# Layer 0's last two groups of MLP tiles by seven quarter products, the modulation columns moved between the groups, and a new order of the seven

## The chip, the cores and the metric

One core of a Trainium2 chip runs the whole kernel. The metric is the device time of one execution in microseconds; the core's five engines are TensorE (PE in the profile), VectorE (DVE), ScalarE (ACT), GpSimd (POOL) and SyncE (SP, which issues all loads here). Each engine works through its own list of instructions in the order in which the list was written, and waits on semaphores for the others.

## The reference, cut to what matters

Two layers, each with a mixer and an MLP, over a sequence of 512 positions of width 1024 in float32. The change touches the MLP and the modulation vectors that both sub-layers use:

```python
for l in range(DEPTH):
    mod = c_act @ w_ada[l] + b_ada[l]              # 6 vectors of 1024 per layer
    ...
    h = rms_norm(x, g_pre_mlp[l]) * (1 + sc_mlp) + sh_mlp
    f = jnp.square(jax.nn.relu(h @ w_ff1[l])) @ w_ff2[l]   # 1024 -> 4096 -> 1024
    x = x + gt_mlp * rms_norm(f, g_post_mlp[l])
```

## The kernel before, in words

Activations lie transposed: 128 features on the partitions, 512 positions along the row. A float32 product is made of three passes in a rounded format: every operand is split into a high part (a cast on ACT) and a low part (the difference, on DVE or POOL), and `passes` (L193 to L200) issues high x high (L198), high x low (L199) and low x high (L200). One block of weights is 128 x 1024 and serves eight 128 x 128 pieces, so a tile of 128 outputs from 1024 inputs is 24 matmuls of 512 columns. `wblock` loads a block (`raw`), casts it on ACT (`whi`, L190) and subtracts on POOL (`wlo`, L191); four buffers `w` hold two blocks' high and low parts.

The MLP (function `mlp`) goes through the 32 tiles of the first product in groups. After the tiles of a group (ff1) comes the second product over just these tiles (ff2): eight tiles `y[m]`, which the first group writes and the later ones add to. `f_out` (L788 to L793) turns a tile into its squared relu and splits it: relu on ACT (L790), square on DVE (L791), high part on ACT (L792), low part on DVE (L793). The bank of PSUM that held the tile is free for PE after L793. There are three banks `mm`, two `cv`, two `ax` and one `cx`.

In layer 0 there are two groups of 16 tiles, all plain. In layer 1 there are four groups of 8, and groups 1 to 3 take their tiles in pairs by `pair_out`: a Strassen-Winograd scheme with seven products of quarter size (256 columns, four 128-blocks deep, 12 matmuls each, so 84 per pair) in place of eight. Its inputs are seven combinations of the quarters of the pair's weights, made by DVE and POOL and split into `wq` tiles (in the same four `w` buffers), and combinations of the activations' quarters, `ta` and `tb`, which `quarters` (L799 to L815) makes once, on DVE, behind the last first-product tile of the group before; its reads and sums go L804 to L810, its split through L174 (ACT) and L175 (DVE). In `pair_out` the banks are `bx` (products w1, then w2 onto it), `ba` (w6), `bb` (w5, then w3 onto it) and `bc` (w7, then w4 onto it); `p1`, `u2` and `q5` are the running sums (L851, L853, L855), and four calls of `f_out` end the pair.

Beside the layer 0 MLP the kernel makes 56 columns of the modulation vectors on DVE: `some(n)` pops n of them, and `ada_col` loads 128 x 1024 numbers (`adr`, three buffers) and reduces them against `cbc` (L293), always behind the last instruction noted in `last[0]`. Before, a first-product tile has one column beside it and a second-product tile two. The last eight second-product tiles' last block is left to `finish`, whose weights are loaded ahead into `slot` buffers (25 in all, one of them held by `cbc` until the last column).

The order on each engine comes from a scheduler with priorities; blocks of weights carry a higher priority (`WPRI`), so their casts are placed early among the other work of ACT. `behind` adds an order without a semaphore.

Of the kernel before, what the change touches and what calls it, by code (L numbers as in the profile page):

```python
# [53 lines left out]
def trunk(ctx, tc, xT, vecs, bg, cst, ccol, crow, wadn, wadt, win, win0, wqkv, wgate, wout, wff1, wff2, yT):  # L54
# [17 lines left out]
    NB = 7  # L72
    GROUPS = [[(16, (1, 2)), (16, (1, 2))], [(8, (0, 0))] * 4]
    SEVEN = [9, 1]
    S2 = 5
# [711 lines left out]
    def mlp(l, hp, pre):  # L787
# [28 lines left out]
        def wq(src, lo_eng):  # L816
            t = wpool.tile([P, 2, T], F32, name="wq", tag="w", bufs=WBUF)
            split(t, src, lo_eng=lo_eng)
            return t

        def pair_out(m, pm, pm1):

            with tc.high_priority(offset=WPRI):
# [11 lines left out]
                w5 = wq(s1, dve)  # L835
                w2 = wq(a12, pool)
                s3, s4 = s2(), s2()
                pool.tensor_tensor(s3, a11, a21, op=ALU.subtract)
                w7 = wq(s3, pool)
                dve.tensor_tensor(s4, a12, s2p, op=ALU.subtract)  # L840
                w3 = wq(s4, pool)
                w4 = wq(a22, pool)

# [11 lines left out]
            dve.tensor_tensor(q5, bb, u2, op=ALU.add)  # L855
            prod(bx, w2, hp[4:8], h0, True)
            f_out(bx, pm, h0)
            prod(bc, w7, ta, h1)
            dve.tensor_tensor(ba, bc, q5, op=ALU.add)
            f_out(ba, pm1, h1)  # L860
            prod(bb, w3, hp[4:8], h1, True)
            dve.tensor_tensor(bb, bb, u2, op=ALU.add)
            f_out(bb, pm, h1)
            prod(bc, w4, tb, h1, True)
            dve.tensor_tensor(bc, bc, u2, op=ALU.add)
            f_out(bc, pm1, h0)

        y, base = None, 0
        for g, (size, rate) in enumerate(GROUPS[l]):
            fp = []  # L870
            if g == 0:
# [6 lines left out]
            for m in range(len(fp), size):  # L878
                if g >= SEVEN[l]:
                    if m % 2 == 0:  # L880
                        fp += [slot(), slot()]
                        pair_out(base + m, fp[-2], fp[-1])
                        some(rate[0])
                else:
                    o = gemm([wff1[l, base + m]], hp)
                    fp.append(slot())
                    f_out(o, fp[-1], slice(0, T))
                    some(rate[0])
            if g == SEVEN[l] - 1:
# [5 lines left out]
            if len(parts):  # L895
                for m in range(NF):
# [3 lines left out]
                    else:  # L900
                        last[0] = dve.tensor_tensor(y[m], y[m], o, op=ALU.add)
                    some(rate[1])
            base += size
# [118 lines left out]
```

## Time and profile before

| | us |
|---|---|
| median of 3 runs | 1593.04 (1591.09 to 1594.87) |
| profiled execution | 1588.86 |
| its span | 1587.1 |
| PE busy | 1525.5 (96%) |
| DVE / ACT / POOL busy | 966.9 / 730.6 / 833.4 |
| mean granted clock | 0.988 |

The span is what the trace covers, from the first to the last instruction; 1.8 us of the execution lie outside. The MLP of layer 0 lies at about 460 to 820 us, that of layer 1 at about 1225 to 1580 us.

### The profile page before, as it was taken

To read this page: it belongs to the slowest core of one execution; us is meant where nothing else is said; L and a number is where in the kernel's file an instruction comes from. 1 tells how busy PE (TensorE), PEld (TensorE's weight loads), DVE (VectorE), ACT (ScalarE), POOL (GpSimd) and SP (SyncE) were. 2 spreads that over 40 slices of the span, in tenths; PEclk is the share of its full clock that TensorE was granted. 3 is DMA by queue.
4 is the path that set the end of the run, shared out by engine and by line. 5 is a ranking of instruction groups with operands and counts; after the bars stand their busy time and mean duration, and the time that the engine had idled before them with its cause. 6 is when DMAs were issued, how large, how long until landed. Compare 5 with 4: busy or idle time off the path is not lost.

```text
span 1587.1 us, 22583 instructions
## 1 busy us (share of the span) xinstructions
PE 1525.5 (96%) x8452; PEld 1268.4 (80%) x8452; DVE 966.9 (61%) x1969; ACT 730.6 (46%) x1308; POOL 833.4 (53%) x536
## 2 busy tenths in 40 slices
PE   5999999999999999999999999999999999999997
PEld 4776766678998888888899777676899879898897
DVE  6899998742363521447667999997316356253544
ACT  3364753454463322332463665445355446253462
POOL 0275753256744444445872867335674446464672
PEclk9999999999999999999999999999999999999999
DMA  8524323303413555566630222220241223333241
GB/s 320 189 81 153 133 90 133 133 27 107 146 57 118 186 200 177 194 189 233 228 107 8 80 73 80 93 67 27 93 144 56 81 93 94 97 95 113 82 134 54
DMA packets 56278, 189.00 MB, mean 119 GB/s; under 512 B 6376, under 2 KB 8552, under 8 KB 56168
## 3 DMA queue, kind: packets, MB, share of 16 engines
q1 hardware_dynamic: 56168, 187.56, 35.8%
q8 instruction: 66, 1.08, 0.3%
q14 instruction: 44, 0.36, 0.1%
HBM read 185.44 MB, written 2.10 MB: 118 GB/s over the span
## 4 chain that ended last, share of the span: by engine, by line
PE 77%; DVE 3%; ACT 2%; POOL 1%; issue 1%; DMA 0%; POOLq 0%; ACTq 0%
PE ps_mm L198 23%; PE ps_mm L200 23%; PE ps_mm L199 23%; PE ps_mm L684 2%; PE ps_mm L696 2%; PE ps_ax L338 1%; POOL wlo L191 1%; ACT whi L190 1%; PE ps_ax L266 1%; PE ps_ax L600 0%; PE ps_ax L671 0%; PE ps_ax L364 0%; DVE ps_cv L451 0%; PE ps_ax L725 0%; PE ps_cv L199 0%
## 5 line engine op out<-in xcount | busy, mean ns | idle before, releaser
L191 POOL TENSOR_TENSOR wlo<-raw,whi 128x1024 fp32r<-128x1024 f32 (+1 forms) x192 | 440.8, 2297 | 436.5 <-ACT whi L190 414.8
L198 PE MATMUL ps_mm<-slot,whi 128*128 128x512 f32 (+1 forms) x1440 | 546.5, 381 | 7.3 <-ACT slot L174 3.4
L200 PE MATMUL ps_mm<-slot,wlo 128*128 128x512 f32 (+1 forms) x1440 | 546.6, 380 | 4.8 <-POOL wlo L191 4.7
L199 PE MATMUL ps_mm<-slot,whi 128*128 128x512 f32 (+1 forms) x1440 | 545.2, 379 | 0.0
L190 ACT CAST whi<-raw 128x1024 fp32r<-128x1024 f32 (+1 forms) x192 | 191.2, 996 | 417.4 <-PE ps_mm L199 304.9
L451 DVE SCALAR_TENSOR_TENSOR ps_cv<-slot,vv,ps_cv 128x512 f32<-128x512 f32 x480 | 332.5, 747 | 1.5
L198 PEld LDWEIGHTS ps_mm<-slot,whi 128*128 128x128 f32 x1440 | 271.7, 189 | 67.0 <-issue 4.2
L200 PEld LDWEIGHTS ps_mm<-slot,wlo 128*128 128x128 f32 x1440 | 271.4, 188 | 63.7 <-POOL wlo L191 7.9
L199 PEld LDWEIGHTS ps_mm<-slot,whi 128*128 128x128 f32 x1440 | 271.9, 189 | 58.8 <-issue 5.5
L198 PE MATMUL ps_mm<-slot 128*128 128x256 f32 (+1 forms) x568 | 160.5, 294 | 11.4 <-DVE slot L793 9.2
L199 PE MATMUL ps_mm<-slot 128*128 128x256 f32 (+1 forms) x568 | 162.9, 291 | 0.6 <-DVE slot L944 0.5
L200 PE MATMUL ps_mm<-slot 128*128 128x256 f32 (+1 forms) x568 | 162.4, 290 | 0.0
L791 DVE TENSOR_TENSOR ps_mm<-rl,ps_mm 128x256 f32<-128x256 f32 (+1 forms) x90 | 45.2, 504 | 130.4 <-ACT rl L790 130.3
L198 PEld LDWEIGHTS ps_mm<-slot 128*128 128x128 f32 x568 | 107.1, 192 | 15.0 <-DVE slot L793 10.2
L199 PEld LDWEIGHTS ps_mm<-slot 128*128 128x128 f32 x568 | 109.3, 193 | 3.2 <-DVE slot L944 0.9
L200 PEld LDWEIGHTS ps_mm<-slot 128*128 128x128 f32 x568 | 109.0, 192 | 1.0
L191 POOL TENSOR_TENSOR slot<-raw,slot 128x1024 fp32r<-128x1024 f32 x34 | 86.1, 2559 | 15.6 <-issue 10.1
L166 POOL TENSOR_TENSOR small<-small,mhalf 128x4 f32<-128x4 f32 (+1 forms) x38 | 34.1, 898 | 95.6 <-DVE small L165 90.9
L198 PE MATMUL ps_mm<-slot,wq 128*128 128x256 f32 x288 | 81.1, 283 | 3.1 <-ACT sq L851 3.1
L199 PE MATMUL ps_mm<-slot,wq 128*128 128x256 f32 x288 | 80.2, 280 | 0.0
L200 PE MATMUL ps_mm<-slot,wq 128*128 128x256 f32 x288 | 80.1, 281 | 0.0
L293 DVE CUSTOM_DVE_ANT_0 adr<-adr,cbc,ini 128x1024 f32<-128x1024 f32 x40 | 65.8, 1657 | 22.9 <-DMA adr<-in_wadt 22.9
(249 smaller groups left out, 2220.0 us busy)
## 6 DMA issues: line engine op xcount, KB each, us to landing
raw<-in_wff SPq DMA_DIRECT2D x138, 512.0 KB, 3.6
raw<-in_win SPq DMA_DIRECT2D x58, 512.0 KB, 3.2
adr<-in_wadt SPq DMA_DIRECT2D x56, 512.0 KB, 4.5
raw<-in_wout SPq DMA_DIRECT2D x36, 512.0 KB, 3.6
adr<-in_wadn SPq DMA_DIRECT2D x28, 512.0 KB, 3.9
raw<-in_wqkv SPq DMA_DIRECT2D x24, 256.0 KB, 2.7
slot<-in_wadt SPq DMA_DIRECT2D x8, 512.0 KB, 8.7
raw<-in_win SPq DMA_DIRECT2D x8, 384.0 KB, 7.0
```

The lines of the kernel that those rows point to most:

```text
L166: pool.tensor_tensor(y, u, mhalf[:, 0:n], op=ALU.pow)
L190: act.copy(out=r32(hi), in_=raw)
L191: wlast[0] = (lo_eng or pool).tensor_tensor(r32(lo), raw, hi, op=ALU.subtract)
L198: pe.matmul(out, whi, xh, start=first, stop=False, skip_group_check=more)
L199: pe.matmul(out, whi, xl, start=False, stop=False, skip_group_check=more)
L200: mark[0] = pe.matmul(out, wlo, xh, start=False, stop=last, skip_group_check=more)
L266: pe.matmul(bk[32 * g:32 * g + 32, :], cc[:, k:k + 1].broadcast_to([P, 32]), raw[:, j * T:(j + 1) * T], start=(k < 4), stop=(k >= 4), skip ...
L293: red = dve.tensor_tensor_reduce(raw, raw, cbc, scale, 0.0 if one else ini, ALU.mult, ALU.add, m)
L451: dve.scalar_tensor_tensor(acc, at[i][:, k:k + T], w, acc, op0=ALU.mult, op1=ALU.add)
L684: pe.matmul(sc[:, 0:n], kf[h][:, k, i * P:(i + 1) * P], qf[h][:, k, i * P:T], start=(k == 0), stop=(k == 1))
L696: pe.matmul(o[:, 0:DH + 1], sts[i][:, (j - i) * P:(j - i + 1) * P], vtok[h][:, i, :], start=(i == 0), stop=(i == j))
L791: dve.tensor_tensor(o, rl[:, ts], o, op=ALU.mult)
```

## The change

Layer 0 gets four groups of 8 tiles too; its groups 2 and 3 (16 tiles, eight pairs) go through `pair_out`, and `quarters` runs behind group 1's first product. Each group carries lists of how many columns stand beside each of its tiles: group 0 two beside the one plain tile behind the halves and two beside each of its eight second-product tiles, group 1 two beside each first-product tile and 2, 1, 1, 1, 1, 1, 1, 1 beside the second product's, group 2 none beside the pairs and 2, 2, 2, 2, 2, 2, 1 beside the second product's, group 3 none. In `pair_out`, in both layers, the products are written in the order w1, w6, w5, w7, w2, w4, w3 instead of w1, w6, w5, w2, w7, w3, w4, and POOL's low parts in a matching order.

```diff
-    GROUPS = [[(16, (1, 2)), (16, (1, 2))], [(8, (0, 0))] * 4]
-    SEVEN = [9, 1]
+    GROUPS = [[(8, [2], [2] * 8), (8, [2] * 8, [2] + [1] * 7), (8, [], [2] * 6 + [1]), (8, [], [])], [(8, [], [])] * 4]
+    SEVEN = [2, 1]
...
-                w2 = wq(a12, pool)
                 s3, s4 = s2(), s2()
                 pool.tensor_tensor(s3, a11, a21, op=ALU.subtract)
                 w7 = wq(s3, pool)
                 dve.tensor_tensor(s4, a12, s2p, op=ALU.subtract)
+                w2 = wq(a12, pool)
+                w4 = wq(a22, pool)
                 w3 = wq(s4, pool)
-                w4 = wq(a22, pool)
...
-            prod(bx, w2, hp[4:8], h0, True)
-            f_out(bx, pm, h0)
             prod(bc, w7, ta, h1)
             dve.tensor_tensor(ba, bc, q5, op=ALU.add)
             f_out(ba, pm1, h1)
+            prod(bx, w2, hp[4:8], h0, True)
+            f_out(bx, pm, h0)
+            prod(bc, w4, tb, h1, True)
+            dve.tensor_tensor(bc, bc, u2, op=ALU.add)
+            f_out(bc, pm1, h0)
             prod(bb, w3, hp[4:8], h1, True)
             dve.tensor_tensor(bb, bb, u2, op=ALU.add)
             f_out(bb, pm, h1)
-            prod(bc, w4, tb, h1, True)
-            dve.tensor_tensor(bc, bc, u2, op=ALU.add)
-            f_out(bc, pm1, h0)
```

On ACT, at the passage from the second to the third pair of layer 1's group 1, these rows stand in the kernel before (`rl` is a relu, `wq` a weight's high part, `sq` the copy p1; `ps_mm_12035` is bb and `ps_mm_12036` bc of the second pair, `ps_mm_12186` bx of the third, and `raw_12152` gives w2 of the third):

```order
L790 ACTIVATE rl_12127<-ps_mm_12035 128x256
L174 CAST wq_12170<-raw_12152 128x512
L174 CAST wq_12176<-s2_12173 128x512
L851 COPY sq_12190<-ps_mm_12186 128x256
L790 ACTIVATE rl_12145<-ps_mm_12036 128x256
L792 CAST slot_11997<-ps_mm_12035 128x256
L174 CAST wq_12180<-s2_12174 128x512
L792 CAST slot_11998<-ps_mm_12036 128x256
```

and these in the changed one, at the same passage (`ps_mm_12748` is bc and `ps_mm_12747` bb of the second pair, `wq_12885` is w7 and `wq_12889` w2 of the third):

```order
L174 CAST wq_12885<-s2_12882 128x512
L790 ACTIVATE rl_12839<-ps_mm_12748 128x256
L174 CAST wq_12889<-raw_12864 128x512
L790 ACTIVATE rl_12857<-ps_mm_12747 128x256
L792 CAST slot_12710<-ps_mm_12748 128x256
L792 CAST slot_12709<-ps_mm_12747 128x256
L174 CAST wq_12892<-raw_12865 128x512
L851 COPY sq_12902<-ps_mm_12898 128x256
```

The last relu of a pair and both its high parts now stand behind the next pair's cast of w2, whose buffer was w6's of that same next pair; the copy p1 stands behind them all, where it stood ahead of one relu and both high parts.

On DVE at the same passage, before:

```order
L791 TENSOR_TENSOR ps_mm_12035<-rl_12127,ps_mm_12035 128x256
L833 TENSOR_TENSOR ps_cx_12310<-ps_ax_12309,raw_12305 128x512
L791 TENSOR_TENSOR ps_mm_12036<-rl_12145,ps_mm_12036 128x256
L853 TENSOR_TENSOR sq_12191<-ps_cv_12187,sq_12190 128x256
L793 TENSOR_TENSOR slot_11997<-ps_mm_12035,slot_11997 128x256
L793 TENSOR_TENSOR slot_11998<-ps_mm_12036,slot_11998 128x256
```

and in the changed kernel:

```order
L791 TENSOR_TENSOR ps_mm_12748<-rl_12839,ps_mm_12748 128x256
L833 TENSOR_TENSOR ps_cx_13022<-ps_ax_13021,raw_13017 128x512
L791 TENSOR_TENSOR ps_mm_12747<-rl_12857,ps_mm_12747 128x256
L793 TENSOR_TENSOR slot_12710<-ps_mm_12748,slot_12710 128x256
L793 TENSOR_TENSOR slot_12709<-ps_mm_12747,slot_12709 128x256
L853 TENSOR_TENSOR sq_12903<-ps_cv_12899,sq_12902 128x256
```

The two last low parts (L793) still stand behind both squares (L791); what has changed is which bank comes first, bc now, and that PE's third product of the next pair, w5 now, is the one that is written into the bank that bc leaves (before, that place in PE's list was w2's, into bx's own bank, and w5 came fourth).

On ACT beside the second product of layer 0's group 1, before (its last tiles; `whi` is a block of ff2, `slot` from `raw` a block for `finish`):

```order
L190 CAST whi_6213<-raw_6212 128x1024
L190 CAST whi_6251<-raw_6250 128x1024
L190 CAST whi_6289<-raw_6288 128x1024
L190 CAST whi_6327<-raw_6326 128x1024
L190 CAST slot_6440<-raw_6439 128x1024
L190 CAST whi_6365<-raw_6364 128x1024
L190 CAST slot_6446<-raw_6445 128x1024
L190 CAST slot_6452<-raw_6451 128x1024
L190 CAST whi_6403<-raw_6402 128x1024
```

and in the changed kernel beside group 1's ff2 (`slot` from `ps_ax` or `ps_cx` is a high part of `quarters`; `whi_5491`, `whi_5526`, `whi_5561` and `whi_5596` are the blocks of y tiles 4, 5, 6 and 7):

```order
L174 CAST slot_5292<-ps_ax_5286 128x512
L190 CAST whi_5491<-raw_5490 128x1024
L174 CAST slot_5295<-ps_cx_5287 128x512
L190 CAST whi_5526<-raw_5525 128x1024
L174 CAST slot_5308<-ps_ax_5302 128x512
L174 CAST slot_5311<-ps_cx_5303 128x512
L174 CAST slot_5324<-ps_ax_5318 128x512
L190 CAST whi_5561<-raw_5560 128x1024
L174 CAST slot_5327<-ps_cx_5319 128x512
L830 COPY ps_ax_5635<-raw_5632 128x512
L174 CAST slot_5340<-ps_ax_5334 128x512
L174 CAST slot_5343<-ps_cx_5335 128x512
```

The casts of ff2's blocks, which stood behind one another alone, now stand behind casts that wait for what DVE makes in `quarters`; on DVE these operations stand among the columns' reductions and the additions to y.

## Rows read from the trace of the kernel before

**Rows 1.** The page: busy time by engine, and the chain that ended last by engine.

```profile
PE 1525.5 (96%) x8452; PEld 1268.4 (80%) x8452; DVE 966.9 (61%) x1969; ACT 730.6 (46%) x1308; POOL 833.4 (53%) x536
...
PE 77%; DVE 3%; ACT 2%; POOL 1%; issue 1%; DMA 0%; POOLq 0%; ACTq 0%
```

**Rows 2.** The waits of PE over the whole span: engine, tile and line that waited, what released it, microseconds in total, times, the longest.

```profile
PE ps_mm L198 <- DVE slot L793: 9.2, 5, 2.9
PE ps_mm L200 <- POOL wlo L191: 4.7, 5, 2.1
...
PE ps_mm L198 <- ACT sq L851: 3.1, 3, 1.0
```

**Rows 3.** Busy time of the engines in two stretches: layer 0's group 1, second product with two columns per tile, and one group of four pairs in layer 1 (stretch, length, busy time with the count of instructions for PE, PEld, DVE, ACT, POOL, granted clock, share of the DMA engines, GB/s).

```profile
724.00:770.00 46.00, 43.85 (x196) 35.32 (x195) 41.82 (x39) 13.34 (x15) 33.18 (x11) 1.00 0.78 272
1312.30:1353.60 41.30, 40.27 (x337) 39.82 (x336) 26.01 (x60) 28.17 (x63) 29.22 (x22) 1.00 0.33 103
```

**Rows 4.** Timeline of ACT at two plain first-product tiles of layer 0.

```profile
501.29 1.05 ACT L190 CAST whi<-raw 128x1024 fp32r<-128x1024 f32 x1 [3.25 <-PE ps_mm L199]
502.24 0.59 ACT L790 ACTIVATE rl<-ps_mm 128x512 f32<-128x512 f32 x1
503.60 0.59 ACT L792 CAST slot<-ps_mm 128x512 fp32r<-128x512 f32 x1 [0.76 <-DVE ps_mm L791]
...
507.80 0.59 ACT L790 ACTIVATE rl<-ps_mm 128x512 f32<-128x512 f32 x1
```

**Rows 5.** Timeline of PE at the second pair of layer 1's group 1 (start, duration, instruction, in brackets the idle time before it and its releaser).

```profile
1324.94 0.28 PE L200 MATMUL ps_mm<-slot,wq 128*128 128x256 f32 x1
1326.25 0.38 PE L198 MATMUL ps_mm<-slot,wq 128*128 128x256 f32 x1 [1.03 <-ACT sq L851]
1326.47 0.28 PE L199 MATMUL ps_mm<-slot,wq 128*128 128x256 f32 x1
...
1327.53 0.28 PE L199 MATMUL ps_mm<-slot,wq 128*128 128x256 f32 x1
```

**Rows 6.** Timeline of PE at the last tile of group 1's second product in layer 0.

```profile
765.49 0.28 PE L199 MATMUL ps_mm<-slot 128*128 128x256 f32 x1
767.88 0.50 PE L200 MATMUL ps_mm<-slot,wlo 128*128 128x512 f32 x1 [2.10 <-POOL wlo L191]
768.21 0.39 PE L198 MATMUL ps_mm<-slot,whi 128*128 128x512 f32 x1
```

**Rows 7.** Timeline of PE at the end of a product between the second and third pair of layer 1's group 1.

```profile
1337.79 0.28 PE L200 MATMUL ps_mm<-slot,wq 128*128 128x256 f32 x1
```

**Rows 8.** Timeline of ACT in the same stretch.

```profile
1338.16 0.62 ACT L174 CAST wq<-raw 128x512 fp32r<-128x512 f32 x1 [0.74 <-PE ps_mm L200]
1338.69 0.38 ACT L790 ACTIVATE rl<-ps_mm 128x256 f32<-128x256 f32 x1
1339.56 0.37 ACT L792 CAST slot<-ps_mm 128x256 fp32r<-128x256 f32 x1 [0.49 <-DVE ps_mm L791]
```

**Rows 9.** Timeline of DVE in the same stretch.

```profile
1339.10 0.43 DVE L791 TENSOR_TENSOR ps_mm<-rl,ps_mm 128x256 f32<-128x256 f32 x1 [1.22 <-ACT rl L790]
...
1339.97 0.42 DVE L793 TENSOR_TENSOR slot<-ps_mm,slot 128x256 fp32r<-128x256 f32 x1
```

**Rows 10.** Timeline of PE at the passage from layer 1's last pair to `finish`.

```profile
1525.67 0.28 PE L199 MATMUL ps_mm<-slot 128*128 128x256 f32 x1
1527.74 0.39 PE L198 MATMUL ps_mm<-slot 128*128 128x256 f32 x1 [1.79 <-DVE slot L793]
```

**Rows 11.** Timeline of DVE at the same passage.

```profile
1526.93 0.43 DVE L791 TENSOR_TENSOR ps_mm<-rl,ps_mm 128x256 f32<-128x256 f32 x1 [0.62 <-ACT rl L790]
1527.27 0.42 DVE L793 TENSOR_TENSOR slot<-ps_mm,slot 128x256 fp32r<-128x256 f32 x1
```

**Rows 12.** Timeline of DVE in the second product of layer 0's group 1, with two columns per tile.

```profile
729.43 0.69 DVE L901 TENSOR_TENSOR yt<-yt,ps_mm 128x512 f32<-128x512 f32 x1 [0.95 <-PE ps_mm L200]
730.04 1.28 DVE L293 CUSTOM_DVE_ANT_0 adr<-adr,cbc,vv 128x1024 f32<-128x1024 f32 x1
...
731.25 3.43 DVE L293 CUSTOM_DVE_ANT_0 adr<-adr,cbc,vv 128x1024 f32<-128x1024 f32 x1
...
735.03 0.69 DVE L901 TENSOR_TENSOR yt<-yt,ps_mm 128x512 f32<-128x512 f32 x1 [0.35 <-PE ps_mm L200]
```

**Rows 13.** Timeline of POOL in the same stretch.

```profile
724.79 2.41 POOL L191 TENSOR_TENSOR wlo<-raw,whi 128x1024 fp32r<-128x1024 f32 x1 [3.15 <-ACT whi L190]
730.37 3.22 POOL L191 TENSOR_TENSOR wlo<-raw,whi 128x1024 fp32r<-128x1024 f32 x1 [3.17 <-ACT whi L190]
```

**Rows 14.** Timeline of DVE in layer 1's `quarters`, from its first operation to its last.

```profile
1270.39 0.68 DVE L804 TENSOR_TENSOR s<-slot 128x512 f32<-128x512 f32 x1
...
1278.92 1.05 DVE L807 TENSOR_TENSOR ps_ax<-s 128x256 f32<-128x256 f32 x1
1279.88 0.41 DVE L809 TENSOR_TENSOR ps_cx<-s,ps_ax 128x256 f32<-128x256 f32 x1
1280.21 2.29 DVE L808 TENSOR_TENSOR ps_ax<-s,s 128x256 f32<-128x256 f32 x1
...
1288.70 0.68 DVE L175 TENSOR_TENSOR slot<-ps_cx,slot 128x512 fp32r<-128x512 f32 x1
```

**Rows 15.** Timeline of PE where layer 1's second product of group 0 ran beside `quarters`.

```profile
1279.16 0.50 PE L198 MATMUL ps_mm<-slot,whi 128*128 128x512 f32 x1 [0.56 <-ACT whi L190]
```

More of the change, by code (lines that the diff above doesn't have):

```diff
@@ L863, in pair_out @@
             f_out(bb, pm, h1)
-            prod(bc, w4, tb, h1, True)
-            dve.tensor_tensor(bc, bc, u2, op=ALU.add)
-            f_out(bc, pm1, h0)
         y, base = None, 0
-        for g, (size, rate) in enumerate(GROUPS[l]):
-            fp = []
+        for g, (size, beside1, beside2) in enumerate(GROUPS[l]):
+            fp, n1, n2 = [], list(beside1), list(beside2)
             if g == 0:
@@ L882, in mlp @@
                         pair_out(base + m, fp[-2], fp[-1])
-                        some(rate[0])
                 else:
@@ L887, in mlp @@
                     f_out(o, fp[-1], slice(0, T))
-                    some(rate[0])
+                    some(n1.pop(0) if n1 else 0)
             if g == SEVEN[l] - 1:
@@ L901, in mlp @@
                         last[0] = dve.tensor_tensor(y[m], y[m], o, op=ALU.add)
-                    some(rate[1])
+                    some(n2.pop(0) if n2 else 0)
             base += size
```

## The prediction, made before the changed kernel ran

> **What bounds the kernel now.** I read the busy times of the page first: PE works 1525.5 of 1587.1 us, and the chain of waits that ended last is PE for 77% [rows 1]. So a change counts by what it takes from PE's own list, and by the gaps that it opens or closes there. Then the list of PE's waits: it is to be seen that few of them lie in the MLPs, and that three of 1.0 us on the copy p1 and one of 2.1 us on POOL's low part are among them [rows 2]. Then the windows, for who has room beside PE: in layer 0's second product with two columns per tile DVE is busy 41.82 of 46 us and POOL 33.18, in a group of pairs DVE only 26.01 of 41.3 [rows 3]. PE's granted clock is 1.00 in both.
>
> **What is taken from PE.** A plain tile of 24 matmuls comes every 5.56 us (502.24 to 507.80), two of them take 11.12 [rows 4]. A matmul of 256 columns comes every 0.118 us (1326.47 to 1327.53, nine steps), so a pair's 84 take 9.89 [rows 5]. Eight pairs in layer 0 save 8 x 1.23 = 9.8 us.
>
> **Stalls that go.** In layer 1 the second pair of each group waits for p1, since w2's product stands right behind w1's on the same bank. From 1324.94 to 1326.25 is 1.31 where 0.12 is due, and the next start is 0.10 late too [rows 5]: 1.3 each, 3.9 in all. The new order puts w5 and w7 between them, 24 matmuls or 2.8 us, which covers the copy. In layer 0, the last tile of group 1's second product waits for its low part: 765.49 to 767.88 where 0.12 is due [rows 6], 2.3 us. That tile then shared POOL and ACT with the weights for `finish`, which now come two groups later, beside pairs that leave room. So 2.3 more, against which the new second product of group 1 is set below.
>
> **A stall that comes, at each passage from a pair to the next.** By the order rows, ACT now runs: relu of bc, cast of w2 of the next pair, relu of bb, the two high parts; DVE: square of bc, square of bb, low part of bc, low part of bb. The cast waits for a buffer, w6's of the next pair, so for the end of that pair's first product. PE's third product there, w5, goes into the bank that bc leaves, so it waits for the low part of bc. With T as the start of w6's product: its last matmul starts at T + 11 x 0.118 = 1.30 and ends at 1.58; a cast that waits for such an end starts 0.09 later (1337.79 + 0.28 to 1338.16) [rows 7, 8], at T + 1.67. The relu behind it starts 0.53 later, T + 2.20 [rows 8]; the square 0.41 later, T + 2.61 [rows 8, 9]; the low part that stands behind the square 0.34 later, T + 2.95, and ends after 0.42 at T + 3.37, as 1526.93 and 1527.27 show; PE follows 0.05 behind [rows 10, 11]. w5 was due at T + 24 x 0.118 = T + 2.83. So 0.6 of idle, with the late second start of [rows 5] 0.7 us. The first passage of layer 0's group 2 has the relu of bc behind the cast as well: its square at T + 2.61, its high part 0.46 later, its low part 0.41 behind that [rows 8, 9], free at T + 3.95, so 1.2. There are six passages in layer 0 and nine in layer 1: 14 x 0.7 + 1.2 = 11.0 us. In the kernel before, w5 came fourth, 1.4 us later, and was not caught. Bounds: 0, if DVE in fact reaches the low part of bc 0.6 earlier, and 15 x 1.2 = 18, if all are like the first.
>
> The trace shows the relu at 1338.69 starting only behind a cast that had waited 0.74 for PE, and DVE 1.22 idle for that relu [rows 8, 9]. [...]
>
> **Layer 0's group 1, second product.** Beside its eight tiles (8 x 5.56 = 44.5 us) DVE gets `quarters`, which in layer 1 took 1270.39 to 1289.38, 19.0 us with POOL's blocks between, some 15 by its own pieces (16 of 512 columns at 0.6 and 16 of 256 at 0.33 from start to start) [rows 12, 14]; 11 reductions (two left from the last first-product tile), eight additions to y (0.6 each, 729.43 to 730.04) and the first pair's combinations (3). A reduction takes 1.28 us alone and 3.43 beside POOL's low part, whose 2.41 in turn becomes 3.22 [rows 12, 13]: the two exclude each other. So DVE needs 15 + 14 + 5 + 3 = 37 us if none is blocked, and 15 + 38 + 5 + 3 = 61 if all are. The order rows say who waits: the cast of y tile 4's block stands behind a high part of `quarters`, that of tile 6 behind three more. I count from the end of the first product. Ahead of the first such high part DVE has the last tile's own end (relu at 502.24, high part until 504.19 [rows 4], 0.7 for the low part and 0.2 around them: 2.9), five reductions (6.4), five sums (3.0), four half sums (1.3), two additions (1.2) and two of POOL's blocks in the way (5): 20. Then the high part 0.6, the block's cast 1.05 [rows 4] and its low part 2.4: 24, where PE wants it at 4 x 5.56 + 0.5 = 22.7: 1.4 late. For tile 6 DVE has about ten more microseconds of its own and two more blocks of POOL, 34.5; with the same 4.05 that is 38.6, due at 6 x 5.56 + 1.4 + 0.5 = 35.3: 3.3 late; with 0.3 for two late starts 5.0 us. The nearest case, layer 1's same place without reductions, lost 0.56 [rows 15]. Bounds: 0.5, and 16 (61 less 44.5) if all reductions are blocked.
>
> That operations with two inputs in SBUF wait, and one with an input in PSUM does not, shows in `quarters`: the L808 at 1280.21 took 2.29, the L809 before it 0.41 [rows 14]. [...]
>
> **The rest.** Layer 0's `finish` now follows a pair. In layer 1 PE then stood from 1525.67 to 1527.74, 1.95 beyond the due 0.12 [rows 10], released by a low part [rows 11]. With bc closed 1.2 us ahead of the end the wait is some 0.25 shorter, since the low part of bc still stands behind the square of bb: +1.7 in layer 0 and -0.25 in layer 1. Bounds 0 and 2. Tiles with two columns come every 5.60 us (729.43 to 735.03) [rows 12], 0.04 more than plain ones; some 20 more tiles than before have two: +0.7. Elsewhere I cost the columns at nothing: beside group 0's second product and group 1's first DVE has 2 x 1.28 + 1.2 + one block of POOL, about 5 of 5.56 us per tile; if that cover is gone, a bank comes late, which three banks hide for a tile.
>
> **Sum.** -9.8 - 3.9 - 2.3 + 11.0 + 5.0 + 1.7 - 0.25 + 0.7 = +2.2 us. The profiled execution was 1588.86 (its span 1587.1 and 1.8 around it), so 1591.0; the median of the runs is 4.2 above it, so I predict 1595 us, no change that can be told. The measurement of this kernel tells 0.2%, 3.2 us.
>
> **The rivals.**
> - Faster, the passages hidden: the term of 11.0 falls away, because DVE gets to the low part of bc before the square of bb is due. For it: the slip is 0.6 us, small beside a chain of six steps; against it: the order is fixed, and each step has its row. 1595 - 11 = 1584.
> - Slower, DVE overrun in layer 0's group 1: from the point at which over half of the reductions meet POOL's block, DVE ends behind PE, and `quarters` delays the first pair as well; 16 in place of 5, so 1606. For it: 41.82 of 46 us already [rows 3]; against it: blocked reductions there came once per tile, not twice [rows 12].
> - Faster, only what is saved: passages, group 1 and `finish` all hidden but for the 0.7: 1593.0 - 16.0 + 0.7 = 1578. It needs two rows to be misread at once.
> - The change doing nothing for layer 0's pairs, so that a pair costs 11.1 there too, I hold as good as excluded: the 84 matmuls are in the order.
>
> **Chances.** The forecast 0.45, with its own range 1590 to 1600; the hidden passages 0.27; the overrun 0.20; only the savings 0.08. Faster by over 0.2% (below 1589.9): 0.27 + 0.08, less 0.01 for the near edge, 0.34. Within: 0.27, six tenths of the forecast. Slower: 0.20 and the rest of the forecast, 0.39. The range from 1581 to 1605 leaves out the third rival and the far end of the second.
>
> **What would show it.** Right: PE's waits on L851 gone; 15 waits on L793 of about 0.6, each at the 25th matmul of a pair; two waits of 1 to 4 us on a weight's cast or low part in layer 0's group 1 second product; one wait of 1.5 to 2 before layer 0's `finish`. Wrong: groups of four pairs at 39.6 us, so no passage waits; or that second product longer than 55 us; or waits on loads, which I saw no cause for.

## The result, and the profile after

The changed kernel takes 1600.4 us (median of 6 runs, 1597.8 to 1602.2), the kernel before 1591.8 (6 runs): ratio 1.0055, 95% interval 1.0043 to 1.0068. It is slower by more than the 0.2% that a measurement of this kernel tells. I had said 1595, within 1581 to 1605, and no change that can be told; to slower I had given 0.39.

The page of the changed kernel, busy time by engine and the chain that ended last, against [rows 1]:

```profile
PE 1525.7 (95%) x8740; PEld 1276.5 (80%) x8740; DVE 1037.3 (65%) x2121; ACT 760.8 (48%) x1404; POOL 858.6 (54%) x568
...
PE 69%; DVE 6%; ACT 4%; POOL 3%; DMA 2%; issue 1%; POOLq 0%; ACTq 0%; DVEq 0%; SPq 0%
```

PE's busy time is that of before, though eight pairs have fewer columns to do; with modelled ends it does not tell where time went. The chain does: PE's share fell from 77% to 69%, and what was lost there went to DVE, ACT, POOL and loads. The waits of PE (in total, times, longest), against [rows 2]:

```profile
PE ps_mm L198 <- DVE slot L793: 18.7, 16, 2.9
...
PE ps_mm L200 <- POOL wlo L191: 8.2, 8, 3.8
...
PE ps_mm L198 <- ACT whi L190: 2.1, 4, 0.6
```

The waits on L851 are gone. Eleven more are there on L793, and one of 3.8 us on a low part. Stage by stage, from PE's first start of a stage to that of the next:

| stage (us) | before | after |
|---|---|---|
| layer 0's MLP | 362.05 | 368.47 |
| of it the 25 plain tiles up to the first pair (25 x 5.56 = 139.0) | - | 148.94 |
| of it the two groups of pairs (bare: 84 x 4 x 0.1178 = 39.58 each) | - | 44.06, 42.54 |
| layer 1's MLP | 353.76 | 355.40 |
| of it the three groups of pairs | 41.30, 41.25, 41.31 | 43.28, 42.47, 42.54 |
| of it `finish` | 51.54 | 49.73 |
| all else (the same code) | 871.3 | 876.6 |

The spans differ by 13.4 us, the medians by 8.6. The rest is the choice of the profiled executions: before's, 1588.86, lay 2.9 below its median, that of the changed kernel, 1602.24, 1.8 above its own, and the code that is the same differs by 5.3. The MLPs differ by 6.42 + 1.64 = 8.1, and that is what is to be explained.

Where the two new losses stand. First a passage from one pair to the next in layer 1, PE and then DVE (timeline: start, duration, instruction, in brackets the idle time and its releaser):

```profile
1422.32 0.28 PE L200 MATMUL ps_cv<-slot,wq 128*128 128x256 f32 x1
1423.27 0.39 PE L198 MATMUL ps_mm<-slot,wq 128*128 128x256 f32 x1 [0.67 <-DVE slot L793]
1423.49 0.28 PE L199 MATMUL ps_mm<-slot,wq 128*128 128x256 f32 x1
```

```profile
1421.27 0.69 DVE L832 TENSOR_TENSOR ps_ax<-raw,ps_ax 128x512 f32<-128x512 f32 x1
1421.86 0.69 DVE L175 TENSOR_TENSOR wq<-ps_ax,wq 128x512 fp32r<-128x512 f32 x1
1422.46 0.43 DVE L865 TENSOR_TENSOR ps_mm<-ps_mm,sq 128x256 f32<-128x256 f32 x1
1422.80 0.42 DVE L793 TENSOR_TENSOR slot<-ps_mm,slot 128x256 fp32r<-128x256 f32 x1
```

The product before the wait goes to `ps_cv`: it is w6's, PE's first of the pair. So the one that waits is the second, w1, at the 13th matmul, and not the third as I had said. It needs the bank that bx leaves, and the low part that closes bx (1422.80) stands on DVE behind a half sum of the pair after next (L832) and a low part of the next one (L175); bx's high part had been there since 1421.97. All ten waits of 0.67 or more stand there, twelve matmuls behind the first on `ps_cv`. Such a wait costs more than it says: the start comes 0.95 after the one before where 0.12 is due (0.83 lost), the next 0.22 after it (0.10), and the third product starts late again (1424.69, 1424.86, 1425.08: 0.15), 1.1 us in all.

At all ten passages ACT's copy for the pair after next (L830), which stands ahead of bx's high part, waited 0.6 to 1.9 us for a load. At eight of them DVE did not stand still for it. At the other two it did, for 0.64 and 0.71 us, and these are the two longest waits of PE, 1.39 at 659.96 and 1.48 at 1347.20; ACT and DVE at the second:

```profile
1344.57 0.59 ACT L830 COPY ps_ax<-raw 128x512 f32<-128x512 f32 x1 [1.86 <-DMA raw<-in_wff]
1345.20 0.70 DVE L832 TENSOR_TENSOR ps_ax<-raw,ps_ax 128x512 f32<-128x512 f32 x1 [0.71 <-ACT ps_ax L830]
```

Then layer 0's group 1, the second product's tile at 630 us, PE, ACT and POOL:

```profile
630.13 0.50 PE L198 MATMUL ps_mm<-slot,whi 128*128 128x512 f32 x1 [0.58 <-ACT whi L190]
630.47 0.40 PE L199 MATMUL ps_mm<-slot,whi 128*128 128x512 f32 x1
634.65 0.51 PE L200 MATMUL ps_mm<-slot,wlo 128*128 128x512 f32 x1 [3.79 <-POOL wlo L191]
```

```profile
628.54 0.59 ACT L174 CAST slot<-ps_ax 128x512 fp32r<-128x512 f32 x1 [1.74 <-DVE ps_cx L809]
629.03 1.05 ACT L190 CAST whi<-raw 128x1024 fp32r<-128x1024 f32 x1
```

```profile
631.01 1.27 POOL L837 TENSOR_TENSOR s<-raw 128x512 f32<-128x512 f32 x1 [9.12 <-DMA raw<-in_wff]
632.24 2.36 POOL L191 TENSOR_TENSOR wlo<-raw,whi 128x1024 fp32r<-128x1024 f32 x1
```

ACT's cast of the block stands behind a cast of `quarters` that waited 1.74 for DVE: that is the predicted chain. But when the block was cast, at 630.08, POOL stood 0.93 longer at the head of its queue with the first pair's difference (L837), for a load, and took 1.27 for it, before it came to the low part. And the clock fell behind the wait (windows: stretch, length, busy time with counts of PE, PEld, DVE, ACT, POOL, then PE's granted clock):

```profile
630.00:635.00 5.00, 1.09 (x4) 0.60 (x5) 4.97 (x10) 3.27 (x6) 3.58 (x2) 1.00 0.32 112
635.00:640.00 5.00, 5.00 (x16) 3.95 (x15) 4.08 (x4) 0.00 (x0) 2.37 (x1) 0.66 0.41 131
```

### The profile page after: what moved, and what is told of

The parts are those of the page before. It is cut to its first block, busy times and chain, and to the rows that moved or that the text cites. A ratio compares the mean times of both kernels' runs of the same rounds, so it can differ in the third digit from the quotient of the medians.

```text
span 1600.5 us, 23486 instructions
## 1 busy us (share of the span) xinstructions
PE 1525.7 (95%) x8740; PEld 1276.5 (80%) x8740; DVE 1037.3 (65%) x2121; ACT 760.8 (48%) x1404; POOL 858.6 (54%) x568
## 4 chain that ended last, share of the span: by engine, by line
PE 69%; DVE 6%; ACT 4%; POOL 3%; DMA 2%; issue 1%; POOLq 0%; ACTq 0%; DVEq 0%; SPq 0%
PE ps_mm L198 21%; PE ps_mm L199 20%; PE ps_mm L200 20%; PE ps_mm L684 2%; PE ps_mm L696 2%; DMA raw<-in_wff 1%; POOL wq L175 1%; DVE adr L293 1%; PE ps_ax L338 1%; POOL wlo L191 1%; ACT whi L190 1%; DMA adr<-in_wadt 1%; DVE slot L793 1%; ACT wq L174 1%; DVE ps_mm L791 1%
## 5 line engine op out<-in xcount | busy, mean ns | idle before, releaser
L191 POOL TENSOR_TENSOR wlo<-raw,whi 128x1024 fp32r<-128x1024 f32 (+1 forms) x176 | 407.1, 2316 | 375.7 <-ACT whi L190 342.1
L198 PE MATMUL ps_mm<-slot,whi 128*128 128x512 f32 (+1 forms) x1312 | 496.3, 379 | 8.9 <-ACT slot L174 3.4
L200 PE MATMUL ps_mm<-slot,wlo 128*128 128x512 f32 (+1 forms) x1312 | 494.8, 379 | 8.4 <-POOL wlo L191 8.2
L199 PE MATMUL ps_mm<-slot,whi 128*128 128x512 f32 (+1 forms) x1312 | 495.3, 378 | 0.3 <-POOL slot L175 0.3
L190 ACT CAST whi<-raw 128x1024 fp32r<-128x1024 f32 (+1 forms) x176 | 174.8, 993 | 356.7 <-PE ps_mm L199 236.5
L198 PEld LDWEIGHTS ps_mm<-slot,whi 128*128 128x128 f32 x1312 | 247.4, 189 | 64.9 <-ACT whi L190 4.7
L200 PEld LDWEIGHTS ps_mm<-slot,wlo 128*128 128x128 f32 x1312 | 247.5, 189 | 63.7 <-POOL wlo L191 12.9
L199 PEld LDWEIGHTS ps_mm<-slot,whi 128*128 128x128 f32 x1312 | 247.4, 189 | 52.7 <-issue 5.5
L198 PE MATMUL ps_mm<-slot,wq 128*128 128x256 f32 x480 | 136.6, 287 | 9.5 <-DVE slot L793 8.5
L199 PE MATMUL ps_mm<-slot,wq 128*128 128x256 f32 x480 | 133.4, 280 | 0.0
L200 PE MATMUL ps_mm<-slot,wq 128*128 128x256 f32 x480 | 131.0, 281 | 0.0
L198 PEld LDWEIGHTS ps_mm<-slot,wq 128*128 128x128 f32 x480 | 90.2, 188 | 15.0 <-DVE slot L793 14.0
L175 POOL TENSOR_TENSOR wq<-raw,wq 128x512 fp32r<-128x512 f32 x60 | 77.3, 1293 | 27.7 <-ACT wq L174 26.0
L199 PEld LDWEIGHTS ps_mm<-slot,wq 128*128 128x128 f32 x480 | 90.3, 188 | 0.2
L200 PEld LDWEIGHTS ps_mm<-slot,wq 128*128 128x128 f32 x480 | 88.7, 188 | 0.0
```

The costliest lines, as they stand in the source:

```text
L175: (lo_eng or dve).tensor_tensor(lo, src, pair[:, 0, :], op=ALU.subtract)
L190: act.copy(out=r32(hi), in_=raw)
L191: wlast[0] = (lo_eng or pool).tensor_tensor(r32(lo), raw, hi, op=ALU.subtract)
L198: pe.matmul(out, whi, xh, start=first, stop=False, skip_group_check=more)
L199: pe.matmul(out, whi, xl, start=False, stop=False, skip_group_check=more)
L200: mark[0] = pe.matmul(out, wlo, xh, start=False, stop=last, skip_group_check=more)
```

## The experiments

A letter stands for the same theory in all expectations. A is the step of the prediction: with the new order a passage waits for a bank that is closed too late. D is the chain in layer 0's group 1: blocks' casts behind the casts of `quarters`. What the others are is said in the expectations. Every run had the kernel before beside it on the same chip, so ratios are compared.

**The order undone, the order alone, another bank, other columns.**

`e1_old_order`: the changed kernel with the products and low parts in before's order, in both layers.

```diff
             dve.tensor_tensor(q5, bb, u2, op=ALU.add)
+            prod(bx, w2, hp[4:8], h0, True)
+            f_out(bx, pm, h0)
             prod(bc, w7, ta, h1)
...
-            prod(bx, w2, hp[4:8], h0, True)
-            f_out(bx, pm, h0)
+            prod(bb, w3, hp[4:8], h1, True)
+            dve.tensor_tensor(bb, bb, u2, op=ALU.add)
+            f_out(bb, pm, h1)
             prod(bc, w4, tb, h1, True)
...
```

> The changed kernel with the old order of the seven products and of their low parts, in both layers; groups and columns stay as changed. Theory A (the new order makes the passage from pair to pair wait for the bank that bc leaves): the five groups of four pairs go back from 42.5 to 44.1 us each to 41.3 (with the wait for the copy p1 of 1.0 us once per group), 8.4 us in all, so about 1592 to 1594 us and no waits of 0.67 on L793 inside the groups. Rival B (the passages wait whatever the order, because DVE and ACT are late in closing a pair): 1599 to 1601, with the waits still there.

Measured 1596.61, ratio 1.0034 (1.0021 to 1.0046). Groups of pairs 40.95 and 41.58 in layer 0, 41.38 to 41.50 in layer 1; the L851 waits are back:

```profile
PE ps_mm L200 <- POOL wlo L191: 6.7, 6, 3.8
PE ps_mm L198 <- ACT sq L851: 4.5, 5, 1.0
```

So the new order costs this kernel some 0.2% (the two intervals just overlap), and without it 0.34% is still lost: the wait of 3.8 does not hang on the order. A's groups of 41.3 came, its 1592 to 1594 did not.

`e2_order_alone`: the kernel before with the new order, so layer 0 untouched.

```diff
-            prod(bx, w2, hp[4:8], h0, True)
-            f_out(bx, pm, h0)
             prod(bc, w7, ta, h1)
...
+            prod(bx, w2, hp[4:8], h0, True)
+            f_out(bx, pm, h0)
```

> The kernel before with only the new order of the products and low parts (layer 1's three groups). Theory A: each group from 41.3 to about 42.5 to 43.3 us, +4.4 in all, less 0.3 to 1.8 at the passage to finish: 1594 to 1596 us. Rival C (the order is a gain, and all of the loss comes from layer 0): the three waits for p1 go and nothing comes, 1587 to 1589.

Measured 1592.92, ratio 1.0014 (1.0003 to 1.0026), within what counts as no change. Groups 42.54, 43.08 and 42.85 where before has 41.3: what the three L851 waits gave is paid back, and more, by nine passages. The time lies 1.1 us below A's range, and above that of C.

`e3_bank`: in the changed kernel ba and bb exchange their pools of banks.

```diff
-            bx, ba, bb, bc = (bank(t)[:, 0:T // 2] for t in ("mm", "cv", "mm", "mm"))
+            bx, ba, bb, bc = (bank(t)[:, 0:T // 2] for t in ("mm", "mm", "cv", "mm"))
```

> The changed kernel with the banks of two accumulators exchanged: ba (w6) takes one of the three mm banks, bb (w5, w3) one of the two cv banks, so that w5 no longer waits for the bank that bc leaves. Theory A: no wait on L793 at the third product, groups of 39.6 to 40.6 us, 17 us above the bare matmuls become 0 to 5: 1584 to 1590 us. Rival B: the closing of a pair is late by itself and the next user of a bank waits instead, groups stay at 42 us or more: 1597 to 1601.

Measured 1598.76, ratio 1.0048 (1.0033 to 1.0064). The scheduler put w5's product first on PE, and the waits on L793 turned into waits on that product's weight:

```profile
PE ps_cv L198 <- ACT wq L174: 7.0, 10, 1.5
```

A's 1584 to 1590 did not come; groups took 41.8 to 43.9. Since the order on PE changed too, it does not tell the theories apart: at a passage something is late whichever bank comes first.

`e4_cols`: no columns beside group 1's second product, more beside group 2 and the pairs.

```diff
-    GROUPS = [[(8, [2], [2] * 8), (8, [2] * 8, [2] + [1] * 7), (8, [], [2] * 6 + [1]), (8, [], [])], [(8, [], [])] * 4]
+    GROUPS = [[(8, [2], [2] * 8), (8, [2] * 8, []), (8, [1] * 4, [2] * 8), (8, [1] * 2, [])], [(8, [], [])] * 4]
...
+                        some(n1.pop(0) if n1 else 0)
```

> The changed kernel with no modulation column beside the second product of layer 0's group 1; the nine columns stand beside pairs of group 2 (four), beside its second product (three more) and beside pairs of group 3 (two). Theory D (reductions together with the quarter sums make DVE late, and the casts behind them): the wait of 3.8 us there and the dip of the clock behind it go, 4 to 7 us less, 0 to 2 given back beside the pairs: 1594 to 1597 us. Rival E (the quarter sums alone make the casts late): the wait stays above 2 us, 1598 to 1601.

Measured 1602.82, ratio 1.007 (1.0055 to 1.0084). The plain stretch fell from 148.94 to 144.59, with waits of 1.11 and 1.63 in place of 3.79; but group 3 of the pairs took 49.62, and D's 1594 to 1597 did not come. ACT, DVE and PE at that group's first wait:

```profile
731.72 0.59 ACT L830 COPY ps_ax<-raw 128x512 f32<-128x512 f32 x1 [6.34 <-DMA raw<-in_wff]
732.34 0.70 DVE L832 TENSOR_TENSOR ps_ax<-raw,ps_ax 128x512 f32<-128x512 f32 x1 [2.53 <-ACT ps_ax L830]
734.51 0.36 PE L198 MATMUL ps_mm<-slot,wq 128*128 128x256 f32 x1 [1.12 <-DVE yt L901]
```

and at its longest:

```profile
760.19 0.38 PE L198 MATMUL ps_mm<-slot,wq 128*128 128x256 f32 x1 [2.34 <-DVE slot L793]
```

The addition to y that PE waits for at 734.51 (L901) stands on DVE behind the half sum of 732.34, which waited for ACT's copy, and that for a load; ahead of the wait at 760.19 the half sum waited 1.79 for a copy, and that 2.36 for a load. So the pairs' weights came late, beside columns' loads that SP issued at 723.38 and 727.38, ahead of and behind one of theirs at 725.07. The reductions take DVE too (1.57 and 2.29 us behind the first of these places); the two were not tried apart.

**Is it ACT's cast of w2?** `e5_cast`: the cast of w2 stands behind the high part of bc of the pair before, so the relus no longer stand behind it.

```diff
+                c2 = act.copy(out=r32(w2[:, 0, :]), in_=a12)
+                if shut[0] is not None:
+                    behind(c2, shut[0])
...
-            f_out(bc, pm1, h0)
+            shut[0] = f_out(bc, pm1, h0)
```

> The changed kernel, new order and banks kept; only ACT's high part of w2 of a pair is put behind the high part of bc of the pair before (an order of issue on one engine, no wait between engines). Theory A (relu and high parts stand behind a cast that waits for PE, and w5 waits for the bank that they close): no wait above 0.2 us at the third product, each of the five groups of pairs from 42.5 to 44.1 us to 39.6 to 40.8, 10 to 14 us less in all: 1587 to 1591 us. Rival B (the next thing in line is as late, the weights of w5 as in the run with exchanged banks): groups stay at 42, 1597 to 1600.

Measured 1600.25, ratio 1.0061 (1.0046 to 1.0076). The passage waits stay, at the same place in the pair. PE:

```profile
1417.36 0.28 PE L200 MATMUL ps_cv<-slot,wq 128*128 128x256 f32 x1
1418.36 0.38 PE L198 MATMUL ps_mm<-slot,wq 128*128 128x256 f32 x1 [0.73 <-DVE slot L793]
```

and ACT, where the cast of w2 (L842) now starts only after PE has gone on:

```profile
1418.94 0.62 ACT L842 CAST wq<-raw 128x512 fp32r<-128x512 f32 x1
```

So the cause that I had named falls. The product that waits is w1, as told above.

**The quarters earlier.** `e6_early` puts `quarters` beside group 0's second product, and the columns elsewhere; `e7_early_old` is that with the old order (the edit of `e1_old_order`), `e8_early_cast` that with the edit of `e5_cast`.

```diff
-    GROUPS = [[(8, [2], [2] * 8), (8, [2] * 8, [2] + [1] * 7), (8, [], [2] * 6 + [1]), (8, [], [])], [(8, [], [])] * 4]
+    GROUPS = [[(8, [2], [0] * 4 + [1] * 4), (8, [2] * 8, [2] * 8), (8, [], [3] * 2 + [2] * 6), (8, [], [])], [(8, [], [])] * 4]
...
-            if g == SEVEN[l] - 1:
+            if g == 0:
                 quarters(last[0])
```

> The changed kernel with the quarter sums of layer 0 made beside group 0's second product (where layer 1 has them too) with only four columns beside them, two columns beside each tile of group 1 and 18 beside group 2's second product. Theory D (quarter sums and reductions in one stage make DVE late and hold up the casts): the wait of 3.8 us and those of 0.5 beside it shrink to about 0.6 in all, and the stretch of 25 plain tiles goes from 148.9 to 141 to 143 us: 1592 to 1595. Rival G (DVE and POOL are as full beside the reductions alone, the lateness moves to the tiles with two and three columns): 1598 to 1601.

> The run before with the old order of the seven products as well. Theories A and D together: groups of pairs at 41.4 us (old wait for p1), plain tiles at 141 to 143: 8 us less by the groups and 6 to 8 by the tiles than the changed kernel, 1586 to 1591, about the kernel before or a little faster. If either theory is wrong, 1593 to 1597.

> Early quarter sums and the cast behind bc's high part together, in the new order. Theories A and D: 16 to 20 us less than the changed kernel, 1580 to 1584, faster than the kernel before by 0.4 to 0.7%. If the cast's place is not what holds the passages: 1592 to 1595.

Measured 1613.22 (1.0146, 1.0129 to 1.0163), 1603.04 (1.008, 1.0066 to 1.0094) and 1609.1 (1.0117, 1.0099 to 1.0135). The plain stretch falls to 144.0 to 145.5 in all three (from 148.94, or 147.3 in `e1_old_order` and `e5_cast`, whose code there is the changed kernel's), so `quarters` does cost some 2 to 5 us there. But the columns that had to go somewhere are now beside the tiles right ahead of the pairs, and layer 0's groups take 48.64 and 50.23 (`e6_early`), 46.25 and 45.67 (`e7_early_old`), 47.93 and 48.77 (`e8_early_cast`). One row of `e6_early`:

```profile
753.46 0.58 PE L198 MATMUL ps_mm<-slot,wq 128*128 128x256 f32 x1 [2.34 <-DVE slot L793]
```

There too the half sum ahead (749.53) had waited 1.40 for a copy, and that 2.26 for a load. In these runs a column cost least beside a plain tile that is not right ahead of the pairs; how much of the rest is its reduction on DVE and how much the late loads stays open.

**Closings and preparation.** `e9_bx`: the copy and the half sum of a pair stand behind the closing of bx of the pair two before. `e10_whi`: in layer 0's group 1 the last eight casts of `quarters` stand behind the casts of the blocks. `e11_both`: both.

```diff
+                c1 = act.copy(out=s1, in_=a21)
+                if len(shut) > 1:
+                    behind(c1, shut[-2][0])
...
+                d1 = dve.tensor_tensor(s1, a22, s1, op=ALU.add)
+                if len(shut) > 1:
+                    behind(d1, shut[-2][1])
...
+            shut.append(f_out(bx, pm, h0))
```

```diff
+                    if l == 0 and g == 1 and m >= 4:
+                        for c in casts[2 * m - 8:2 * m - 6]:
+                            behind(c, wcast[0])
```

> The changed kernel, with the copy of A21 (L830) and the first half sum (L832) of each pair placed behind the high and the low part of the tile that bx holds in the pair two before. Theory A2 (the product that waits at a passage is w1, the second, since bx's bank is closed by DVE behind the preparation of the pair that comes two later): the waits of 0.67 on L793 at the 13th matmul go or fall below 0.3, groups of four pairs take 39.8 to 41.2 us where they took 42.5 to 44.1, and the time is 1585 to 1592. Rival F (DVE has simply too much to do beside a pair, so that what is moved back makes a weight late in place of the bank): groups stay at 42 or more, with waits on L174 or L175, and the time is 1597 to 1603. The scheduler puts w2 ahead of w7 in two of the three following pairs, which under either theory may bring back a wait on L851 of up to 0.3 per pair. The wait of 3.8 us in layer 0's group 1 is not touched and should stay.

> The changed kernel, with ACT's casts of the quarters of layer 0 (eight of 16, those beside y tiles 4 to 7) placed behind the cast of that tile's block of weights. Theory D (the wait of 3.8 us on the low part of y tile 6's block comes from that block's cast, which stands on ACT behind casts of quarters that wait for DVE's sums): the wait falls to 1.0 or less, the plain part of layer 0 takes 142 to 145 us where it took 148.9, and the time is 1593 to 1597. Rival G (it is POOL's low part itself that DVE's reductions and sums lock out, wherever ACT's cast stands): a wait of 2.5 or more remains, the plain part stays at 147 or more, and the time is 1598 to 1602. The passages are not touched: waits of 0.67 and groups of 42.5 to 44 under both.

> Both edits together: the copy and half sum behind bx's end, and the block's casts ahead of the quarters' casts in layer 0's group 1. If A2 and D both hold, the gains add, about -11 and -5: 1581 to 1588, faster than the kernel before. If one of the rivals F and G holds, 1590 to 1597; if both, 1598 to 1603. If the two gains do not add (the lost time only moves to a later wait of the same engine), the sum is short of the two single ones by more than 3 us.

`e9_bx` measured 1606.51, ratio 1.0096 (1.0078 to 1.0113): slower, against A2's 1585 to 1592. Groups 43.7 in layer 1, 44.2 and 43.8 in layer 0. The second product now starts nearly in time (1424.46, 0.35 after the start before it); the third waits instead, PE and DVE:

```profile
1425.87 0.28 PE L200 MATMUL ps_mm<-slot,wq 128*128 128x256 f32 x1
1426.82 0.39 PE L198 MATMUL ps_mm<-slot,wq 128*128 128x256 f32 x1 [0.67 <-DVE slot L793]
```

```profile
1424.32 0.69 DVE L835 TENSOR_TENSOR ps_ax<-raw,ps_ax 128x512 f32<-128x512 f32 x1
1424.92 0.93 DVE L791 TENSOR_TENSOR ps_mm<-rl,ps_mm 128x256 f32<-128x256 f32 x2
1425.75 0.69 DVE L838 TENSOR_TENSOR ps_cx<-ps_ax,raw 128x512 f32<-128x512 f32 x1
1426.35 0.75 DVE L793 TENSOR_TENSOR slot<-ps_mm,slot 128x256 fp32r<-128x256 f32 x2
```

The half sum and the sum behind it (L835, L838) had left the place ahead of bx's closing and stood ahead of the next two. It looks like the rival F; but no weight was late (no wait of 0.25 or more on a `wq`), so it was the order still, and not too much work.

`e10_whi` measured 1597.44, ratio 1.0035 (1.0023 to 1.0048). The wait fell from 3.79 to 1.59, the plain stretch from 148.94 (147.3 in `e1_old_order`, `e5_cast` and `e9_bx`, with the same code there) to 142.69, and the clock behind that wait stays at full speed:

```profile
635.00:640.00 5.00, 5.00 (x27) 4.22 (x26) 4.88 (x8) 0.72 (x2) 1.19 (x2) 1.00 0.68 221
```

What is left of the wait, on ACT and POOL: the block's cast at 630.41 stands behind the first pair's copy (L832), which waited 1.81 for DVE.

```profile
629.89 0.59 ACT L832 COPY ps_ax<-raw 128x512 f32<-128x512 f32 x1 [1.81 <-DVE slot L815]
630.41 1.05 ACT L190 CAST whi<-raw 128x1024 fp32r<-128x1024 f32 x1
```

```profile
631.54 2.37 POOL L191 TENSOR_TENSOR wlo<-raw,whi 128x1024 fp32r<-128x1024 f32 x1 [1.14 <-ACT whi L190]
```

D holds for the stretch (142 to 145 us expected) and misses by a little in time (1593 to 1597) and in the wait, which did not fall to 1.0. The time shows only half of what the stretch gained, 3 us: the first group of pairs behind it took 47.08 where it took 44.06, with a wait of 1.78 at its first passage (1.39 in the changed kernel) and PE's clock low behind that:

```profile
655.00:660.00 5.00, 5.00 (x30) 4.70 (x29) 1.86 (x5) 2.17 (x5) 2.71 (x3) 0.66 0.45 140
```

`e11_both` measured 1603.36, ratio 1.0068 (1.0048 to 1.0089): what `e10_whi` gains and what `e9_bx` loses add up.

`e13_last`: as `e11_both`, but the copy and the half sum stand behind the last closing of the pair two before, that of bb.

```diff
-            shut.append(f_out(bx, pm, h0))
+            f_out(bx, pm, h0)
...
-            f_out(bb, pm, h1)
+            shut.append(f_out(bb, pm, h1))
```

> Both edits of before, but the copy and the half sum of each pair placed behind the last closing of the pair two before (the high and the low part of bb), and not behind that of bx; so the two sums L835 and L838, which stood ahead of bc's and bb's closing in the kernel with both edits, stand behind them, and the order of the seven on PE is the changed kernel's again. Theory A3 (at a passage DVE and ACT close three banks and prepare the pair after next in the same four microseconds; any preparation ahead of a closing makes PE wait at the product that takes that bank, and the weights themselves are not urgent, being needed 10 us later): the waits of 0.4 to 0.95 on L793 fall below 0.3, groups of four pairs take 39.9 to 41.0 us where they took 43.7, no wait on L174 or L175 in the pairs, and the time is 1583 to 1590, faster than the kernel before. Rival F (DVE and ACT have too much to do beside a pair, so the preparation becomes late in its turn): waits on L174 or L175 of 0.3 or more at w6 or w5, groups at 42 or more, time 1596 to 1604.

Measured 1591.32 (11 runs) beside 1590.17 (15 runs), ratio 1.0008 (0.9999 to 1.0017): no change from the kernel before, and 0.6% better than `e11_both`, which has the same instructions in another order. The passage waits are gone but for one of 0.96 in layer 0. PE's waits on L793, then PE and DVE at a passage:

```profile
PE ps_mm L198 <- DVE slot L793: 11.2, 7, 2.9
```

```profile
1423.27 0.28 PE L200 MATMUL ps_cv<-slot,wq 128*128 128x256 f32 x1
1423.62 0.39 PE L198 MATMUL ps_mm<-slot,wq 128*128 128x256 f32 x1
...
1425.03 0.28 PE L200 MATMUL ps_mm<-slot,wq 128*128 128x256 f32 x1
1425.39 0.39 PE L198 MATMUL ps_mm<-slot,wq 128*128 128x256 f32 x1
```

```profile
1424.58 0.43 DVE L791 TENSOR_TENSOR ps_mm<-rl,ps_mm 128x256 f32<-128x256 f32 x1 [0.67 <-ACT rl L790]
1424.91 0.96 DVE L793 TENSOR_TENSOR slot<-ps_mm,slot 128x256 fp32r<-128x256 f32 x2
1425.94 0.70 DVE L837 TENSOR_TENSOR ps_ax<-raw,ps_ax 128x512 f32<-128x512 f32 x1
1426.67 0.70 DVE L840 TENSOR_TENSOR ps_cx<-ps_ax,raw 128x512 f32<-128x512 f32 x1
```

The two sums stand behind the closings, no weight is late there (the one wait on a weight in the pairs is 0.17, at 647.43), and DVE is even idle for 0.67 us. Groups take 41.67, 41.58 and 41.62 in layer 1 and 43.97 and 41.75 in layer 0. A3 is right on the waits and wrong on the size: two late starts remain at every passage (0.35 and 0.36 where 0.12 is due, each with a second one of 0.22), 0.7 us, for a reason that no run here shows, so the groups stayed above the 41.0 expected, and the time is 1.3 us above the expected range. The one that F foretold, 1596 or more, did not come.

## Why the prediction was right or wrong

- **The pairs, -9.8.** Right: 16 plain tiles are 89.0 us, the eight pairs bare 79.2; they save 9.8.
- **The waits on p1, -3.9, and on POOL's low part, -2.3.** Right: both are gone.
- **The passages, +11.0.** Here the step failed. I had w5, the third product, wait for bc's bank, because ACT's relu stands behind the cast of w2. What waits is w1, the second, on bx's bank; `e5_cast` took the cast away and the waits stayed. w2, which stood right behind w1 before [rows 5], is the fifth product now, so bx is closed in the last four microseconds of a pair, together with the banks of the two last products, and DVE has the next pairs' sums and low parts in between. I had followed bc and bb through the order rows and not bx. That the price per wait (0.6) came out nearly right for the wrong product and the wrong bank is luck; the cost is higher, 1.1 where the wait is 0.67, with its late starts. In layer 0 the two groups stand 7.4 above bare, where my term for them was 5 x 0.7 + 1.2 = 4.7; in layer 1 the groups grew by 4.4, where my terms gave 9 x 0.7 - 3.9 = 2.4. `e9_bx` and `e13_last` show the cause by order: moving the copy and the half sum moves the wait from the second product to the third, and with the same instructions as `e11_both`, but behind all closings, all are gone but one of 0.96. Both engines' orders, ACT's copy and DVE's half sum, were moved together; at the passage shown DVE came last. The late loads lengthened two of the ten.
- **Group 1's second product, +5.0 (with 0.7 for two columns 5.7).** Mis-sized: the plain stretch is 9.9 above its bare 139.0. Of that 1.5 lie beside group 0's second product (waits of 0.49 at 515.88 and 0.44 at 517.05), where I had the columns at nothing, and 8.4 beside group 1's. There the chain is the predicted one, waits behind casts of `quarters` at the tiles that I named; tile 4's was smaller than said (0.38 at 618.61 for 1.4), tile 6's larger (0.58 + 3.79 for 3.3), and one of 0.49 at 606.52 I had not named. Two things were missing in the step: POOL's queue, in which the first pair's difference and its late load stand ahead of the low part, and the clock, 0.66 for the five microseconds behind the wait (a third of 5, some 1.7 us). `e10_whi` took 4.6 to 6.2 of the 9.9 away by eight casts' places, and gave 3.0 back in the group of pairs behind. That the load behind L837 costs its 0.93 is read from the trace; it was not tried alone.
- **Layer 0's `finish`, +1.7.** Right: PE waits 1.63 at 779.97. **Layer 1's, -0.25**: the wait went from 1.79 [rows 10] to 1.62, right; that the stage shrank by 1.8 is for the rest the clock, below, which the prediction had no term for.
- **What was to be seen.** No wait on L851: right. Fifteen waits of 0.6 at the 25th matmul: ten of 0.67 or more at the 13th; at each group's third passage only two late starts of 0.35 and 0.37. Waits on loads: I saw no cause; PE itself waited for none, but POOL did ahead of the low part of tile 6, and ACT's copies at the passages.

Sum: 5.9 us more in the MLPs than the +2.2 of the prediction. 4.2 of it is the plain stretch (2.7 in group 1's second product, 1.5 in group 0's), 4.8 the passages; some 3 us come back, 1.6 of them in layer 1's `finish`, which is luck. Between the medians the change is 8.6; the 1595 stood 1.2 us nearer, because the median of three runs that it was set on (1593.04) lies that much above that of six (1591.8). The overrun that I held as rival, 1606 by group 1 alone, did not come: the place was right, and its price is nearer to the forecast's 5 than to the rival's 16. The time lies between the two.

The sum for the passages rests on the order in which ACT and DVE take their work. At the passage of the order rows both ran as listed in the changed kernel: on ACT w7's cast at 1345.84, a relu at 1346.37, w2's cast at 1346.64, the other relu at 1347.15; on DVE the squares at 1347.07 and 1347.99, the low parts from 1348.32. And the place in it counts: a group of layer 1 took 43.7 us with the copy and the half sum behind bx's closing (`e9_bx`), 41.6 with both behind that of bb (`e13_last`).

No version beats the kernel before: the 9.8 us saved in layer 0 are paid for by passages (some 2.0 us a group even in `e13_last`, 4.4 in the first), the plain stretch (142.7 against 139.0 there) and layer 0's `finish`.

## What to carry to other kernels

When an order of products is changed, list for every bank where it is closed and where it is needed next, and look at what else the closing engine has in its queue in between; the bank that loses most need not be the one that the edit names. Preparation that is needed ten microseconds later belongs behind a closing that is needed at once, and a step that frees one bank by moving work ahead of another only moves the wait. Price a wait with its late starts: a shown wait of 0.67 us cost 1.1.

## What the runs showed of the hardware that I had not expected

PE's granted clock fell to 0.66 in the stretch (635 to 640) behind one stand in which PE had been busy 1.09 of 5 us: in part of it starts of 512 columns came 0.42 us apart (635.33 to 635.75) where 0.23 is usual (638.64 to 638.87). With a stand of 1.59 in the same tile, in `e10_whi`, it stayed at 1.00, and fell to 0.66 in the same run behind one of 1.78 (655 to 660, above). And layer 1's `finish` began at a lower clock before, and not after, with the kernel's own wait ahead of it nearly the same (1.79 and 1.62). The five microseconds from PE's start behind that wait, in the kernel before and then in the changed one:

```profile
1527.50:1532.50 5.00, 4.76 (x27) 4.76 (x28) 0.72 (x3) 2.84 (x4) 5.00 (x3) 0.66 0.60 161
```

```profile
1542.70:1547.70 5.00, 4.93 (x41) 4.94 (x42) 0.86 (x3) 1.87 (x4) 5.00 (x4) 1.00 0.63 178
```

Behind the stand of 2.10 in layer 0 of the kernel before [rows 6] the clock stayed at 1.00 (768 to 773), so the length of the stand alone does not tell it; why it fell in the one place and not in the other stays open. Code that was not touched differed by 5.3 us between the two profiled executions, so a few microseconds in one stage are not to be read as the effect of an edit.
